# The down projection of narrow second tiles in plain float32 on groups of array columns

## The chip, the cores and the metric

The kernel runs on one core of a Trainium2 chip. The metric is the device time of one execution in microseconds (us), the median of several runs. Profiles are of one execution taken by the hardware profiler. Engines: PE is TensorE (PEld its weight loads), DVE is VectorE, ACT is ScalarE, POOL is GpSimd, SP is SyncE, which issues most of the transfers.

## The reference

One layer of a decoder over 4096 tokens of width 1024 in float32: a norm, a combined input projection, two groups of heads (gated DeltaNet and retention), an output projection with residual, and then a mixture of experts with residual and a last norm. The change lies in the mixture of experts alone:

```python
# top-1 group of 8, then top-2 of its 8 experts; 64 experts of width 256
gate = lax.ragged_dot(xs, w_gate, group_sizes)
up = lax.ragged_dot(xs, w_up, group_sizes)
y = lax.ragged_dot((jax.nn.silu(gate) * up).astype(xs.dtype), w_down, group_sizes)
y = y * weights[order].astype(y.dtype)[:, None]
out = jnp.zeros_like(ht).at[tok].add(y)
```

`w_down` is 256 x 1024 for each expert, so the contraction of the down projection has two slices of 128.

## The kernel before

The kernel runs through the mixer (both groups of heads), then `post` (the rest of the output projection, the router and a table of each expert's tokens), and last `moe`, the expert stage, from about 2700 us on.

Each expert has a fixed number of rows: the experts are ranked by their token counts, and rank r of either class gets `CAPS[r]` rows, from 256 down to 76. An expert with more than 128 rows has two tiles of rows, the first with 128 and the second with the rest. The second tiles have 128, 104, 84, 68, 60, 52, 48, 40, 32, 28, 24, 20, 16, 12, 8, 6, 4 and 2 rows, each size twice (one expert in each class). So 28 second tiles have at most 64 rows: 8 have 40 to 60, and 20 have 2 to 32.

The stage is written out by hand in rounds, one per expert e (`tc.manual_schedule()`, the loop at line 1650; the letters of `LOOP = "AFCDNBEGIMHJLO"` give the order). Every engine takes its instructions in that order. In round e, c is expert e, n is e+1, m is e+2, p is e-1 and q is e-2:

- A gathers the tokens of e+3 (POOL's queue); F gathers the rows of `out` of p (`gather_y`, POOL's queue).
- C and I are the gate and up products of c (`up`, line 1582), plain float32 with tiles of weights stationary and the tokens moving.
- D adds q's result (`add`), squares it on ScalarE (`square`), and has GpSimd take the power (`rms`); G norms and scatters it (`store`).
- B and H transpose n's first and second tile (`turn`, line 1512, with a product on VectorE at line 1514).
- N and E are the activation of c and p: `tanh`, then `silu`, which leaves h split into two float32r tiles `hh` and `hl`.
- M scales m's tokens on ScalarE. L prepares tables.
- J splits c's down weights: `split` (line 1399) makes `dh` on ScalarE and `dl` on VectorE from the raw float32 tile `dn`, then `fetch_dn(e)` asks for the down weights of expert e+2.
- O is the down projection of p: `down` (line 1517) for each tile.

`Rows.down` takes two halves of 512 output columns. For each one `mm3` (line 933) issues three float32r products (hh x dh, hh x dl, hl x dh) for each of the two slices of the contraction, with the tokens' h stationary (128 rows of the array by R columns) and 512 weights moving; the result `y` is a PSUM tile of one bank, of which there are two, and ScalarE evacuates it into `ys` with the token's weight as scale (line 1525). The product of one tile therefore has 12 float32r products and two evacuations.

The raw down weights `dn` have two buffers (`NDN = 2`, 1 MB per expert): those of e+2 take the buffer of e as soon as it is split. The gate and up weights `gu` have five buffers of half an expert; a load waits until the up product that read the buffer is through (line 1394). Both kinds are issued on SyncE's queue, in the order of the program.

Of the kernel before, what the change touches and what calls it, by code (L numbers as in the profile page):

```python
# [17 lines left out]
P = 128  # L18
# [55 lines left out]
def mixer(tc, outer, banks, x, attn_norm, w_in, conv_a, a_log, dt_bias, norm_a, norm_b, cst, rope, mixed, clear, w_out, x1):  # L74
    """Both groups of heads. While the last chains of products run out, the first row blocks of the output
    projection take the room between them; returns that projection, to go on with."""
# [6 lines left out]
    with ExitStack() as ctx:  # L83
# [23 lines left out]
        # a pair of heads of the first kind takes 16 units of projections, so does one of the second  # L107
# [16 lines left out]
        def fetch(m):  # L124
            """A quarter of 256 columns of weights: two of the eight slices."""
            if m < len(quarters):
                src, c0, n, k = quarters[m]
                W = src.shape[-1]
                raws[m] = wp.tile([P, 2, 264], F32, name="wr", bufs=NWR)
                nc.sync.dma_start(raws[m][:, :, :n], rows(src, c0 + k * 2 * P * W, [[W, P], [P * W, 2], [1, n]]))  # L130
# [16 lines left out]
        class Lane:  # L147
            """Chains that run beside the projections, a step at a time."""
# [38 lines left out]
        def unit(u, evac, kind):  # L187
            """After unit u of four of a group of projections."""
            g = gi[0]
            act = dict(L=la.tick, E=evac or (lambda: None), T=later, S=lambda: split(4 * g + 5 + u), B=behind)  # L190
            for o in STEPS[kind]:
                act[o]()
            if u == 3:
                gi[0] += 1
# [77 lines left out]
        # normalised, transposed and split input rows  # L272
# [33 lines left out]
        def x_prep(r):  # L306
            """Closures for the ticks that bring in row block r."""
            box = []
            return [lambda: box.append(x_norm(r)), lambda: box[0] and box[0]()]
# [47 lines left out]
        with tc.manual_schedule():  # L357
# [26 lines left out]
            def setup(i):  # L384
                """What the first units of projections need and come with."""
# [14 lines left out]
            for sb in range(NS):  # L400
# [4 lines left out]
                for kind, pr in stages:  # L405
# [3 lines left out]
                    if kind == "a":  # L409
                        # gate (and, with the first pair, beta and alpha)  # L410
# [22 lines left out]
                        # q, k, v with conv and SiLU (times two), channels on partitions  # L433
# [50 lines left out]
class Out:  # L484
    """The output projection and the residual, a block of rows at a time."""
# [30 lines left out]
    def half(self, r, h):  # L516
        """Half of the columns; a generator of two steps."""
# [30 lines left out]
    def units(self, n):  # L548
        """The first n blocks, as far as they are asked for. At the end of a block the next one is turned, and of the
        one after it the first operand loaded."""  # L550
# [29 lines left out]
# order of the work around a unit of projections: L a step of the chain of the first kind, E the unit's own  # L580
# results, T what waits for other engines, S the next weights, B small things in the background
STEPS = dict(g="LTBES", h="LBST", t="ELSTB", r="EBLTS", v="SBLET", y="LETSB")
# steps of that chain at each unit, for both pairs of heads
# [5 lines left out]
def zero(nc, t, zt, i, n):  # L589
    """Fill the i-th of n parts of a DRAM tensor with zeros."""  # L590
# [5 lines left out]
def gdn_pair(tc, sb, pr, co, gcd, gs, qkv, ready, L):  # L596
# [81 lines left out]
    # inverse of the unit upper triangular matrices: the diagonal blocks by substitution, NQ partitions to a block  # L678
    # with one of NQ rows in turn each, ...
# [49 lines left out]
    # ... then by block doubling  # L729
# [25 lines left out]
    # sequential part  # L755
# [120 lines left out]
# The groups are dealt to two classes by their number of tokens, and the experts of a class ranked by theirs.  # L876
# An expert of one class follows one of the other, so that a token's two experts are never neighbours.
# Rows kept for the expert of rank r in its class; what exceeds them takes the loop at the end.
# a round of the loop over the experts, and the last rounds; the sizes of the pairs of experts: b big, s small
# [6 lines left out]
def pairs():  # L886
    """Ranks in both classes, in the order of the work: large and small ones in turn, small ones at the end."""
# [38 lines left out]
class Split:  # L926
    """hi/lo halves (12 bits each) of a float32 operand."""
# [13 lines left out]
class Shared:  # L941
    """Constants of the router and of the experts, and what the one finds out for the other."""
# [33 lines left out]
def post(tc, out, wrg, wre, sh, tab, then):  # L976
    """The rest of the output projection, router, and the table of each expert's tokens."""
    nc = tc.nc
    NR = out.x.shape[-2] // P
    with ExitStack() as ctx:  # L980
# [13 lines left out]
        with tc.manual_schedule():  # L994
# [7 lines left out]
            # blocks are turned for the router two at a time until they have caught up  # L1002
# [47 lines left out]
            def turn_x(end):  # L1050
# [16 lines left out]
                # the last four in twos  # L1067
# [37 lines left out]
def route(tc, t0, n, S, sh, rst, xT, wr, usb, oneb, oacc, oaf, tab, scat, pools):  # L1105
    """Groups, experts and weights of n blocks of tokens, entered in the table; a generator of its steps."""
# [27 lines left out]
    def top(v, other):  # L1134
        """The largest of eight, its place counted from the end (the first one wins) and mask; other work between."""
# [12 lines left out]
    def exps(v):  # L1148
        """One over the sum of the exponentials of v less its largest, as work for top()."""
# [88 lines left out]
def counts(nc, psm, oneb, oacc):  # L1238
    """Tokens of each expert, along the rows and down a column."""
# [6 lines left out]
def place(sh, cr, key):  # L1246
    """An expert's rank in its class by what cr and key hold, and its place in the order."""
# [9 lines left out]
def classes(tc, sh, oneb, oacc, psm, sp):  # L1257
    """Classes of the groups, and the experts that come first, from the tokens so far; a generator of its steps."""
# [8 lines left out]
    # class of each group by its rank: 0 1 1 0 0 1 1 0  # L1267
# [26 lines left out]
    # the largest and the smallest keep their places  # L1294
# [13 lines left out]
def rank(tc, sh, oneb, oacc, psm, sp):  # L1308
    """Experts by falling count."""
# [21 lines left out]
def beyond(nc, sh, info, ptr):  # L1331
    """The list of tiles beyond the fixed ones: expert, first row."""
    C, io, q = sh.C, sh.io, sh.q
    cc = lambda i: q[:, i:i + 1]
    # tiles over the capacity, first of them
# [26 lines left out]
def moe(tc, w_gate, w_up, w_down, sh, x1, tab, info, out):  # L1362
    """The experts; a generator that leaves off once the first weights are asked for."""
# [5 lines left out]
    NX, NGU, NDN = 12, 5, 2  # L1369
    assert max(sum(NTILE[i:i + 6]) for i in range(NEXP)) <= NX  # L1370
    with ExitStack() as ctx:
# [6 lines left out]
        class Weights:  # L1378
            """An expert's weights, loaded in thirds."""
# [35 lines left out]
        def fetch_dn(e):  # L1415
            while dq and dq[0] <= e + NDN:
                W[dq.pop(0)].fetch(2)
# [3 lines left out]
        fetch_dn(-1)  # L1421
# [7 lines left out]
        def meta(M, n, selfkey, mask):  # L1429
            """Gather and scatter indices and scales of n tiles from their table rows."""  # L1430
# [12 lines left out]
            # the partner's place and capacity, and whether it lies beyond that  # L1443
# [11 lines left out]
            # second: the token's other expert comes before this one  # L1455
# [7 lines left out]
            # a first row stays scaled until it is stored  # L1463
# [22 lines left out]
        class Rows:  # L1486
            """Up to 128 tokens of an expert. A token's first expert leaves y + x1 in out, its second one
            adds to that and normalises."""
# [28 lines left out]
            def down(self, w, h, o):  # L1517
                R = self.R
                self.y = ap.tile([P, D], F32, name="ys")
                for c in range(2):  # L1520
# [3 lines left out]
                                     Split(w.hi[:, k, s], w.lo[:, k, s])) for k in range(2)])  # L1524
# [37 lines left out]
        class Expert:  # L1562
# [30 lines left out]
            def silu(self):  # L1593
# [6 lines left out]
                self.h = Split(hi, lo)  # L1600

            def down(self):
                for i, t in enumerate(self.tiles):
                    t.down(self.w.dn, self.h, i * P)
# [19 lines left out]
        with tc.manual_schedule():  # L1624
# [25 lines left out]
            for e in range(NEXP + 2):  # L1650
# [20 lines left out]
                def down_weights():  # L1671
                    c.w.split()
                    fetch_dn(e)

                def aside():
                    if e >= 8:
                        next(extra, None)
                    if e - e % G + G < NEXP:
                        if e % G < 4:
                            next(pend)  # L1680
                        elif e % G == 4:
# [5 lines left out]
                             M=(m, lambda: m.each("scale")), N=(c, lambda: c.tanh()), O=(p, lambda: p.down()))  # L1687
# [82 lines left out]
```

## Time and profile before

| | |
|---|---|
| time, median of 3 runs | 3663.53 us (3661.81 to 3665.11) |
| span of the profiled execution | 3669.7 us (the profile gives no other time for it) |
| TensorE busy | 3431.1 us, 93% |
| VectorE busy | 2415.7 us, 66% |
| ScalarE busy | 1716.0 us, 47% |
| GpSimd busy | 1140.5 us, 31% |
| DMA traffic | 573.55 MB, mean 156 GB/s |
| mean granted clock of TensorE | 0.977 |

The span runs from the first to the last instruction. Busy times are over the whole span; the expert stage has other shares than the mixer, so the stage is read from windows. Matmuls are pipelined, and a matmul's duration in a row goes on beyond the start of the next one: what a product takes on TensorE is read from the distance between starts. A plain float32 product appears as two weight loads and two matmuls, a float32r one as one of each.

### The profile page before, as it was taken

To read this page: it belongs to the slowest core of one execution; us is meant where nothing else is said; L and a number is where in the kernel's file an instruction comes from. 1 tells how busy PE (TensorE), PEld (TensorE's weight loads), DVE (VectorE), ACT (ScalarE), POOL (GpSimd) and SP (SyncE) were. 2 spreads that over 40 slices of the span, in tenths; PEclk is the share of its full clock that TensorE was granted. 3 is DMA by queue.
4 is the path that set the end of the run, shared out by engine and by line. 5 is a ranking of instruction groups with operands and counts; after the bars stand their busy time and mean duration, and the time that the engine had idled before them with its cause. 6 is when DMAs were issued, how large, how long until landed. Compare 5 with 4: busy or idle time off the path is not lost. (4 is left out here: it accounts for less than half of the span.)

```text
span 3669.7 us, 66531 instructions
## 1 busy us (share of the span) xinstructions
PE 3431.1 (93%) x24177; PEld 3137.1 (85%) x24177; DVE 2415.7 (66%) x6134; ACT 1716.0 (47%) x3706; POOL 1140.5 (31%) x1384
## 2 busy tenths in 40 slices
PE   7999999999999999999998999999969999999997
PEld 6888888888898888998988988888858888888885
DVE  6677677677677677677676664443546667777765
ACT  4345344344344444444444432222236666776775
POOL 1322332332232232232341320211123444444453
PEclk9999999999999999999999999999979999999998
DMA  5435335335344344353353335333267898999996
GB/s 139 116 84 141 85 87 139 86 100 126 87 121 110 82 121 105 82 132 98 85 122 100 86 98 168 110 116 103 82 199 251 285 307 295 310 309 335 345 308 196
DMA packets 565562, 573.55 MB, mean 156 GB/s; under 512 B 202560, under 2 KB 508272, under 8 KB 565232
## 3 DMA queue, kind: packets, MB, share of 16 engines
q1 hardware_dynamic: 528864, 484.51, 45.5%
q0 software_dynamic: 34976, 84.20, 6.5%
q8 instruction: 192, 3.15, 0.3%
q14 instruction: 138, 1.13, 0.1%
q10 hardware_dynamic: 1392, 0.56, 0.1%
HBM read 498.09 MB, written 102.56 MB: 164 GB/s over the span
## 5 line engine op out<-in xcount | busy, mean ns | idle before, releaser
L217 PE MATMUL acc<-wh,hh 128*128 128x256 f32 (+1 forms) x2560 | 764.8, 299 | 106.0 <-ACT rv L821 70.5
L219 PE MATMUL acc<-wh,hl 128*128 128x256 f32 (+1 forms) x2560 | 737.4, 288 | 2.4 <-DVE hl L297 2.4
L218 PE MATMUL acc<-wl,hh 128*128 128x256 f32 (+1 forms) x2560 | 737.5, 288 | 0.3 <-DVE wl L142 0.2
L217 PEld LDWEIGHTS acc<-wh,hh 128*128 128x128 f32 x2560 | 500.6, 196 | 116.3 <-ACT rv L821 73.8
L219 PEld LDWEIGHTS acc<-wh,hl 128*128 128x128 f32 x2560 | 500.2, 195 | 3.1 <-DVE hl L297 3.1
L218 PEld LDWEIGHTS acc<-wl,hh 128*128 128x128 f32 x2560 | 501.2, 196 | 1.0 <-DVE wl L142 0.8
L141 ACT ACTIVATE wh<-wr 128x512 fp32r<-128x512 f32 (+1 forms) x520 | 319.3, 626 | 252.0 <-DMA wr<-in_w_in_dram 247.5
L142 DVE TENSOR_TENSOR wl<-wr,wh 128x512 fp32r<-128x512 f32 (+1 forms) x520 | 388.0, 750 | 56.6 <-ACT wh L141 50.8
L205 PE MATMUL acc<-hh,wh 128*128 128x512 f32 x768 | 317.2, 413 | 0.0
L207 PE MATMUL acc<-hh,wl 128*128 128x512 f32 x768 | 303.3, 395 | 0.0
L206 PE MATMUL acc<-hl,wh 128*128 128x512 f32 x768 | 302.1, 393 | 0.0
L1582 PEld LDWEIGHTS g<-xT,gu 128*128 128x128 f32 x2048 | 273.4, 193 | 18.7 <-DVE xT L1514 9.2
L1582 PE MATMUL g<-xT,gu 128*128 128x128 f32 (+30 forms) x2048 | 279.1, 295 | 6.1 <-DVE xT L1514 6.0
L1582 PE MATMUL u<-xT,gu 128*128 128x128 f32 (+30 forms) x2048 | 275.6, 293 | 0.0
L1582 PEld LDWEIGHTS u<-xT,gu 128*128 128x128 f32 x2048 | 266.1, 191 | 1.9
L253 POOL TENSOR_TENSOR gs<-gs,nrow 128x256 f32<-128x256 f32 x128 | 118.6, 929 | 394.9 <-DVE gs L252 394.9
L245 DVE SCALAR_TENSOR_TENSOR cv<-xin,pcol,cv 128x512 f32<-128x512 f32 x288 | 216.0, 750 | 6.8
L810 POOL TENSOR_TENSOR rqk<-rqk,rb 128x256 f32<-128x256 f32 x128 | 118.3, 924 | 272.6 <-DVE rb L809 196.4
L1557 POOL DMA_INDIRECT out_dram<-xg,mi x100 | 130.4, 1304 | 188.9 <-DVE ss L1553 96.3
L1525 ACT ACTIVATE ys<-y,mf 128x512 f32<-128x512 f32 (+22 forms) x200 | 133.6, 679 | 113.8 <-PE y L938 100.7
L936 PE MATMUL y<-dh,hh 128*128 128x512 f32 (+16 forms) x400 | 164.6, 412 | 22.6 <-ACT ys L1525 13.8
L1528 POOL DMA_INDIRECT xg<-out_dram,mi x97 | 97.0, 1001 | 256.2 <-PE tr L1512 43.9
(367 smaller groups left out, 8143.3 us busy)
## 6 DMA issues: line engine op xcount, KB each, us to landing
wr<-in_w_in_dram SPq DMA_DIRECT2D x480, 256.0 KB
gu<-in_w_gate_dram SPq DMA_DIRECT2D x128, 512.0 KB
gu<-in_w_up_dram SPq DMA_DIRECT2D x128, 512.0 KB
dn<-in_w_down_dram SPq DMA_DIRECT2D x64, 1024.0 KB
xi<-in_x_dram SPq DMA_DIRECT2D x64, 512.0 KB
mixed<-mx SPq DMA_DIRECT2D x128, 128.0 KB
out_dram<-zt SPq DMA_DIRECT2D x8, 2048.0 KB
xi<-mixed SPq DMA_DIRECT2D x32, 512.0 KB
```

The costliest lines, as they stand in the source:

```text
L141: nc.scalar.activation(h, r, AF.Copy)
L142: nc.vector.tensor_tensor(l, r, h.bitcast(F32), op=OP.subtract)
L205: nc.tensor.matmul(a, wh[:, s], hh[:, k, :], start=(k == 0), stop=False)
L206: nc.tensor.matmul(a, wh[:, s], hl[:, k, :], start=False, stop=False)
L207: nc.tensor.matmul(a, wl[:, s], hh[:, k, :], start=False, stop=(k == KC - 1))
L217: nc.tensor.matmul(a[:, :n], hh[:, k, s], wh[:, :n], start=(k == 0), stop=False)
L218: nc.tensor.matmul(a[:, :n], hh[:, k, s], wl[:, :n], start=False, stop=False)
L219: nc.tensor.matmul(a[:, :n], hl[:, k, s], wh[:, :n], start=False, stop=(k == KC - 1))
L245: nc.vector.scalar_tensor_tensor(cv, xin[:, j:j + T], tap(j), cv, op0=OP.mult, op1=OP.add)
L936: nc.tensor.matmul(out, a.hi, b.hi, start=(i == 0), stop=False)
L1525: nc.scalar.activation(self.y[:R, s], y[:R], AF.Copy, scale=self.f[:R, WT, self.n:self.n + 1])
L1582: nc.tensor.matmul(o[:, b, :R], self.w.gu[k // 4][:, k % 4, i * DE + b * P:i * DE + b * P + P], self.xT[:, k, :R], start=(k == 0), stop=(k ...
```

## The change

For a second tile (`o` is the row offset, 0 for the first tile) of at most 64 rows, the down projection takes h as plain float32 (`h.whole`, the tile that `silu` had split) and the raw float32 weights (`w.raw`). The array's 128 columns are taken as groups of m = 32 (up to 32 rows) or 64 columns, and the 1024 output columns are cut into as many parts of n = 256 or 512. Each part goes to another group of columns, and with it to other partitions of one PSUM tile. Slices of the contraction are the outer loop, groups the inner one. ScalarE evacuates each group from its partitions into the part of `ys`, so four evacuations of 256 columns or two of 512.

First tiles, wider second tiles and the loop for what exceeds the fixed rows run as before, so all down weights are still split. Since the raw weights are read by the down projection, they have three buffers, and the weights of e+2 are asked for after p's down projection instead of after c's split; three experts' down weights are asked for ahead of the stage instead of two.

```diff
-        NX, NGU, NDN = 12, 5, 2
+        NX, NGU, NDN = 12, 5, 3
...
         def fetch_dn(e):
-            while dq and dq[0] <= e + NDN:
+            while dq and dq[0] < e + NDN:
                 W[dq.pop(0)].fetch(2)
...
-        fetch_dn(-1)
+        fetch_dn(0)
...
             def down(self, w, h, o):
                 R = self.R
                 self.y = ap.tile([P, D], F32, name="ys")
+                if o and R <= 64:
+                    m = 32 if R <= 32 else 64
+                    n = D * m // P
+                    y = py.tile([P, T], F32, name="y")
+                    for k in range(2):
+                        for j in range(P // m):
+                            nc.tensor.matmul(y[j * m:j * m + R, :n], h.whole[:, k, o:o + R], w.raw[:, k, j * n:j * n + n],
+                                             start=(k == 0), stop=(k == 1))
+                    for j in range(P // m):
+                        nc.scalar.activation(self.y[:R, j * n:j * n + n], y[j * m:j * m + R, :n], AF.Copy,
+                                             scale=self.f[:R, WT, self.n:self.n + 1])
+                    return
                 for c in range(2):
                     y = py.tile([P, T], F32, name="y")
                     s = slice(c * T, c * T + T)
                     mm3(nc, y[:R], [(Split(h.hi[:, k, o:o + R], h.lo[:, k, o:o + R]),
-                                     Split(w.hi[:, k, s], w.lo[:, k, s])) for k in range(2)])
+                                     Split(w.dn.hi[:, k, s], w.dn.lo[:, k, s])) for k in range(2)])
...
                 self.h = Split(hi, lo)
+                self.h.whole = h
...
             def down(self):
                 for i, t in enumerate(self.tiles):
-                    t.down(self.w.dn, self.h, i * P)
+                    t.down(self.w, self.h, i * P)
...
                 def down_weights():
                     c.w.split()
+                    if not p:
+                        fetch_dn(e)
+
+                def down():
+                    p.down()
                     fetch_dn(e)
...
-                             M=(m, lambda: m.each("scale")), N=(c, lambda: c.tanh()), O=(p, lambda: p.down()))
+                             M=(m, lambda: m.each("scale")), N=(c, lambda: c.tanh()), O=(p, down))
```

## Rows read from the trace of the kernel before

**Rows 1.** Windows: length, busy us (instructions) of each engine, granted clock, DMA share, GB/s.
```profile
2950.00:3159.50 209.50, 207.01 (x1358) 184.22 (x1357) 147.26 (x294) 144.06 (x194) 90.00 (x93) 1.00 0.91 300
3159.50:3594.60 435.10, 419.96 (x2986) 363.73 (x2985) 308.59 (x595) 310.29 (x423) 206.48 (x198) 1.00 0.94 323
3534.80:3538.20 3.40, 3.40 (x10) 2.26 (x9) 3.37 (x7) 2.38 (x4) 2.00 (x2) 0.50 1.09 357
```
**Rows 2.** Waits of PE, 3159.5 to 3594.6: us in total, times, longest.
```profile
PE y L936 <- ACT ys L1525: 8.2, 9, 1.5
PE y L936 <- ACT hh L1598: 5.3, 4, 3.1
```
**Rows 3.** Waits of DVE, 3159.5 to 3594.6.
```profile
DVE ss L1545 <- ACT g L1541: 67.4, 48, 2.4
DVE ss L1553 <- POOL ss L1546: 29.0, 14, 4.8
DVE hl L1599 <- ACT hh L1598: 13.8, 28, 0.5
...
DVE xT L1514 <- PE tr L1512: 3.6, 6, 1.1
```
**Rows 4.** Waits of DVE, 2950 to 3159.5.
```profile
DVE ss L1545 <- ACT g L1541: 29.6, 20, 2.5
...
DVE hl L1599 <- ACT hh L1598: 6.8, 13, 0.6
DVE ss L1553 <- POOL ss L1546: 5.5, 4, 2.8
```
**Rows 5.** Timeline of PE around a 32-row tile: start, us, instruction.
```profile
3172.65 4.51 PE L1582 MATMUL g<-xT,gu 128*128 128x160 f32 x32
3176.99 1.04 PE L1512 MATMUL tr<-cst,xg 128*128 128x128 f32 x8
...
3185.54 0.39 PE L938 MATMUL y<-dh,hl 128*128 128x512 f32 x1
3185.77 0.39 PE L936 MATMUL y<-dh,hh 128*32 128x512 f32 x1
...
3188.32 0.40 PE L938 MATMUL y<-dh,hl 128*32 128x512 f32 x1
3188.55 0.69 PE L1582 MATMUL g<-xT,gu 128*128 128x156 f32 x4
```
**Rows 6.** Groups by form, ACT, 2830 to 3669: xcount, busy us, mean ns, idle before.
```profile
L1525 ACT ACTIVATE ys<-y,mf 32x512 f32<-32x512 f32 x4 | 2.7, 680 | 2.8 <-PE y L938 2.8
...
L1591 ACT ACTIVATE h<-g 128x256 f32<-128x256 f32 x4 | 1.5, 363 | 0.0
```
**Rows 7.** Timeline of PE's weight loads, the same tile.
```profile
3185.55 0.11 PEld L936 LDWEIGHTS y<-dh,hh 128*32 128x32 f32 x1
3185.77 0.11 PEld L937 LDWEIGHTS y<-dl,hh 128*32 128x32 f32 x1
```
**Rows 8.** Timeline of ACT, the same tile.
```profile
3188.75 0.68 ACT L1525 ACTIVATE ys<-y,mf 32x512 f32<-32x512 f32 x1 [0.71 <-PE y L938]
3189.34 1.04 ACT L1541 ACTIVATE g<-xg 128x1024 f32<-128x1024 f32 x1
```
**Rows 9.** Waits of SP's queue, 2830.8 to 3594.6.
```profile
SPq L1394 <- PE u L1582: 313.1, 43, 11.9
SPq L1397 <- DVE dl L1403: 74.7, 23, 6.7
```
**Rows 10.** Timeline of SP's queue around the same tile.
```profile
3187.14 0.38 SPq L1397 DMA_DIRECT2D dn<-in_w_down_dram  x1
3197.04 0.37 SPq L1394 DMA_DIRECT2D gu<-in_w_gate_dram  x1
```
**Rows 11.** Timeline of PE ahead of a stretch at half clock.
```profile
3533.50 0.50 PE L936 MATMUL y<-dh,hh 128*128 128x512 f32 x1 [0.86 <-ACT hh L1598]
```

## Prediction

> **What bounds the kernel now.** The change touches only the expert stage, so I cut the view of windows there first. Narrow second tiles (at most 64 rows) come in two stretches: the 8 of 33 to 64 rows in 2950 to 3159.5 us, the 20 of at most 32 rows in 3159.5 to 3594.6 us, the last just behind it [rows 1]. The reader is to see TensorE busy 207.0 of 209.5 us and 420.0 of 435.1 us, DMA shares of 0.91 and 0.94, VectorE and ScalarE near 70%, and a granted clock of 1.00 in both (2.4 GHz). Next the waits of TensorE in the second stretch: 8.2 us for the evacuation `ys`, 5.3 us for `hh`, hardly anything else, no DMA [rows 2]. So TensorE sets the time, and what it saves is worth something. How much, the waits of VectorE tell. In the second stretch VectorE is busy 308.6 us, and waits 67.4 us for ScalarE's squares, 29.0 us for GpSimd's power and 13.8 us for `hh`, against only 3.6 us for TensorE [rows 3]. The first three are the replies of its own chain (add, square, power, norm), which a shorter product doesn't shorten. 308.6 + 67.4 + 29.0 + 13.8 = 418.8 of 435.1 us: VectorE's chain has about 16 us left before it is the bound. In the first stretch it is 147.3 + 29.6 + 6.8 + 5.5 = 189.2 of 209.5 us, 20 us left [rows 1, 4].
>
> **What is removed.** A narrow tile now takes 12 float32r products of 512 columns. With a 32-row tile the first starts at 3185.77 and the next expert's first product at 3188.55, so 2.78 us, 0.23 us each [rows 5]; there is no gap in it, all of it is on TensorE's path. The two evacuations of 512 columns cost ScalarE 0.68 us each [rows 6], 1.36 us.
>
> **What is added on TensorE.** A plain float32 product runs as two passes: the 16 products of `g` (8 slices, 2 halves) show as x32 [rows 5]. At 160 columns 32 passes take 3176.99 - 3172.65 = 4.34 us, 0.136 us each, so I estimate 0.136 x 256/160 = 0.217 us for 256 columns and 0.434 us for 512.
> - At most 32 rows: 2 slices x 4 groups x 2 passes = 16 passes of 256 columns, 16 x 0.217 = 3.47 us if one follows the other.
> - 33 to 64 rows: 2 x 2 x 2 = 8 passes of 512 columns, 8 x 0.434 = 3.47 us.
>
> So the work is longer by 0.69 us a tile unless passes in different groups of array columns run beside each other. No row of before has two groups at work, so it must be bounded. Upper end: no overlap, 3.47 us. Lower end: all groups together, 2 x 2 passes of one group: 0.87 us at 32 rows, 1.74 us at 64. Between them is the order in which the program issues: both passes of a product stand next to each other and go to the same group. In all rows here products start in program order. If that stays so, a second pass waits for the first of its group, and the first pass of the next group can start only beside it. Then 8 products at 32 rows take 9 steps of 0.217, 1.95 us, and 4 products at 64 rows 5 steps of 0.434, 2.17 us. I take this middle, since start in program order is what the rows show: saved 0.83 x 20 = 16.6 us in the second stretch and 0.61 x 8 = 4.9 us in the first, 21.5 us of TensorE.
>
> Two rules of the Trainium skill speak against the change. Going from 128 to 32 stationary columns and back costs nothing here: 3185.54 to 3185.77 and 3188.32 to 3188.55 are the same 0.23 us [rows 5]. The Trainium skill, "TensorEngine Tiling (Array Packing)", Key Properties, says that a change of the tiling mode drains the engine. Taken as the part of a product that lies beyond its spacing, 0.39 - 0.23 = 0.16 us, twice a tile, that would take 28 x 0.32 = 9.0 us off the saving; going by the row it is 0, and I keep the row, which has no column group other than the first in it. The weight loads of 0.11 us start at 3185.55 and 3185.77, beside products on the same rows of the array [rows 5, 7]. The Trainium skill, "TensorE: Matmul & The Clock Gate", Part 3, The mechanism, lets a load run beside a product only where the row groups differ; here all rows are used, and by it 16 x 0.11 = 1.8 us a tile would come on top. The trace disagrees, and I add nothing.
>
> **What is added elsewhere.** ScalarE: at 32 rows four evacuations of 256 columns take the place of two of 512. The nearest row, 256 columns out of PSUM, is 0.363 us; the other end is 0.68 us [rows 6]. I take 0.45, near the first, so 1.8 against 1.36 us, +0.44 us; range +0.1 to +1.36. It matters only for order: all four can start only after the last pass, where before one of two ran beside the products. Before, the last `ys` starts 0.20 us behind the products (3188.75 against 3188.55), and the next expert's square follows it at 3189.34 [rows 5, 8]. So ScalarE is through 0.20 + 0.68 = 0.88 us behind them, and after the change 0.20 + 4 x 0.45 = 2.00 us, 1.1 us later (two of 512 at 33 to 64 rows: 1.56 us, 0.7 later). Against the earlier end of the products this is 0.3 us lost at 32 rows and 0.1 at 64 for VectorE's chain. PSUM: one `y` buffer instead of two a narrow tile; the wait for the first tile's evacuation (8.2 us, rows 2) stays. ScalarE's and VectorE's splits of the weights stay too, for the first tiles.
>
> The weights' load: with three raw buffers the load for expert e+2 reuses the buffer of e-1, and is issued behind the products of e-1 rather than behind the split of e. SyncE now waits 74.7 us in all for that split (`dl`) [rows 9]. After the change it waits for the end of the down projection instead, at about the same place in a round (the products end at 3188.55, the load went out at 3187.14 [rows 5, 10]), and where the second tile isn't narrow, for nothing. Queued behind it are the next `gu` loads, which wait for `u` anyway (313.1 us, rows 9), at 3197.04, so some 8 us later. Cost 0; what hides it is that this load has nearly two rounds before its split. The third load ahead of the stage moves 1 MB earlier, off the path.
>
> **The sum.** Second stretch: 16.6 us are saved on TensorE, but VectorE's chain has 16 us of room and loses 20 x 0.3 = 6 us of it to the later squares, so 10 us. First stretch: 4.9 us saved, 20 us of room, 8 x 0.1 = 0.8 us lost, so 4 us. Together 14 us. The profiled execution gives its span alone, 3669.7 us; the median of the runs is 6.2 us below it (0.17%). The difference is carried over: 3663.5 - 14 = 3649.5 us.
>
> **Rivals.**
> - Full overlap: 1.91 x 20 + 1.04 x 8 = 46.5 us of TensorE. For it: groups write disjoint PSUM partitions and hold their own weights. Against it: the starts in program order. VectorE's chain caps the second stretch at 16 us, and the first leaves all 8.3 us: 24 us, 3639.5 us. The Trainium skill, "TensorE: Matmul & The Clock Gate", Part 3, Measured speedup vs the span model, gives 2.38 times for three column tiles; no row of before shows it.
> - No overlap, slower: the column groups take turns as products of the whole array do now. Place: every narrow tile. Price 0.69 x 28 = 19.3 us. TensorE's idle time (15 us in the second stretch, rows 1) takes in a few: +16, 3680 us. It decides from an overlap of less than 3.47 / 2.78 = 1.25. For it: no row of before shows two passes at once.
> - The chain of VectorE is already the bound in these rounds: TensorE only waits longer for `hh`; within 3 us of before, 3662 us.
> - The clock: soon after TensorE had waited 0.86 us for `hh` [rows 11], the granted clock stood at 0.50 (1.2 GHz) for 3.4 us [rows 1], which costs 1.7 us. If longer waits bring this in each of the 28 rounds, 48 us go, more than is saved: 3690 us with the saving of the middle case, 3663.5 + 48 - 21.5. Against it: it came once in 644 us.
>
> **How the numbers follow.** Middle case 42%, full overlap 24%, no overlap 20%, chain of VectorE 9%, clock 5%. About 0.2% (7.3 us) can be told from no change. The middle case lies between 4 and 20 us faster and reaches the bound in three of four; full overlap nearly always; no overlap nearly always on the other side. Faster: 0.32 + 0.23 = 0.55; slower: 0.18 + 0.05 = 0.23; the rest, 0.22, within. The range must reach to no overlap on one side and into full overlap on the other: 3633 to 3680 us; the middle case alone is 3644 to 3660.
>
> **What would show it.** In the trace after, a narrow tile's passes: starts 0.217 us apart mean no overlap, pairs at 0.217 us the middle, four starts close together full overlap; first pass to the next expert's `g` in 3.5, 2.0 or 0.9 us. Wrong on the sum if VectorE's waits for TensorE stay at a few us while TensorE's waits for `hh` grow by as much as it saves (VectorE bound), or if stretches at clock 0.50 become frequent, or if `dn` loads are late and ScalarE waits for them.

## The result and the profile after

The kernel after takes 3695.03 us (median; 3691.41 to 3697.2) against 3662.89 us for the one before on the same chip: the ratio is 1.0075, 95% interval 1.0063 to 1.0088. The forecast was 3649.5 us with a range of 3633 to 3680. The sign was wrong and the time lies outside the range.

What the change does on TensorE, it does better than forecast. The timeline of PE around a 32-row tile and a 60-row tile in the kernel after (start, us, instruction; xN counts passes), beside [rows 5]:

```profile
3194.71 0.39 PE L938 MATMUL y<-dh,hl 128*128 128x512 f32 x1
3195.03 1.07 PE L1527 MATMUL y<-dn,h 128*32 128x256 f32 x16
3196.03 2.25 PE L1595 MATMUL g<-xT,gu 128*128 128x156 f32 x15
...
2987.70 0.39 PE L938 MATMUL y<-dh,hl 128*128 128x512 f32 x1
2988.02 1.94 PE L1527 MATMUL y<-dn,h 128*60 128x512 f32 x8
2989.89 3.82 PE L1595 MATMUL g<-xT,gu 128*128 128x104 f32 x32
```

From the wide tile's last product to the next expert's first it is 3196.03 - 3194.71 = 1.32 us (2.19 us for the 60-row tile), where the kernel before needs 3188.55 - 3185.54 = 3.01 us [rows 5]. Where nothing waits, that is 1.69 us saved in each of 20 tiles and 0.82 us in each of 8, 40 us in all. And yet the kernel lost 32 us.

The windows of [rows 1] in the kernel after, and a stretch of 3.3 us further on (length, busy us of PE, PEld, DVE, ACT and POOL, granted clock, DMA share, GB/s). Of TensorE's 435.1 us, 392.8 are busy:

```profile
2950.00:3159.50 209.50, 204.58 (x1341) 178.90 (x1339) 145.70 (x286) 144.93 (x194) 89.90 (x92) 0.99 0.92 303
3159.50:3594.60 435.10, 392.80 (x2970) 346.03 (x2969) 303.17 (x591) 314.94 (x451) 206.07 (x195) 0.97 0.92 316
...
3351.90:3355.20 3.30, 3.23 (x8) 2.56 (x9) 1.75 (x3) 3.21 (x5) 2.13 (x4) 0.50 1.10 358
```

Waits of PE in 3159.5 to 3594.6 us, kernel after (us in total, times, longest), which answer to [rows 2]. The wait for `hh` went from 5.3 to 16.5 us, and waits for `xT`, 0.5 us before, come to 13.8 us:

```profile
PE y L936 <- ACT hh L1611: 16.5, 14, 5.5
PE y L1527 <- ACT ys L1538: 11.6, 11, 1.5
PE tr L1512 <- DVE xT L1514: 6.9, 10, 2.6
PE g L1595 <- DVE xT L1514: 6.9, 7, 2.1
```

Waits of DVE in 3159.5 to 3594.6 us, then in 2950 to 3159.5 us, kernel after, which answer to [rows 3, 4]. VectorE's wait for GpSimd's power is what grew: 29.0 to 46.2 us, and 5.5 to 14.7 us. Its wait for TensorE's transposes, 3.6 us before, is 0.3 us in the second stretch: there VectorE no longer waits for TensorE, TensorE waits for VectorE.

```profile
DVE ss L1558 <- ACT g L1554: 63.8, 49, 2.1
DVE ss L1566 <- POOL ss L1559: 46.2, 19, 5.2
DVE hl L1612 <- ACT hh L1611: 14.9, 30, 0.5
...
DVE xT L1514 <- PE tr L1512: 0.3, 1, 0.3
...
DVE ss L1566 <- POOL ss L1559: 14.7, 5, 4.7
```

Waits of SP's queue in 2830.8 to 3594.6 us, kernel after, which answer to [rows 9]. The down-weight load (L1397) waited 74.7 us for `dl`, the split of this round; now it waits for the end of the narrow products in some rounds, and in most for nothing:

```profile
SPq L1394 <- PE u L1595: 385.6, 47, 16.7
SPq L1397 <- PE y L1527: 68.2, 18, 9.8
SPq L1397 <- DVE dl L1403: 16.4, 3, 6.3
```

One round shows the whole chain. Timelines of SP's queue, POOL, DVE and PE in the kernel after, 3324 to 3352 us (start, us, instruction; in brackets the idle time before it and what the profile infers as its end):

```profile
3324.67 0.37 SPq L1394 DMA_DIRECT2D gu<-in_w_up_dram  x1
3325.29 0.66 SPq L1397 DMA_DIRECT2D dn<-in_w_down_dram  x1
...
3326.26 2.06 POOL L1570 DMA_INDIRECT out_dram<-xg,mi  x1 [1.93 <-DVE xT L1514]
3328.62 1.93 POOL L1501 DMA_INDIRECT xg<-x,mi  x1 [0.30 <-issue]
3336.32 0.99 POOL L1541 DMA_INDIRECT xg<-out_dram,mi  x1 [5.76 <-ACT xg L1505]
3337.62 0.95 POOL L1541 DMA_INDIRECT xg<-out_dram,mi  x1 [0.30 <-ACT dh L1402]
3338.60 0.59 POOL L1559 TENSOR_TENSOR ss<-ss,ex 128x1 f32<-128x1 f32 x1
...
3330.93 0.15 DVE L1558 TENSOR_SCALAR ss<-ss 128x1 f32<-128x1 f32 x1 [1.27 <-ACT g L1554]
3339.22 0.28 DVE L1566 TENSOR_SCALAR ss<-ss,mf 128x1 f32<-128x1 f32 x1 [5.17 <-POOL ss L1559]
3340.74 2.35 DVE L1403 TENSOR_TENSOR dl<-dn,dh 128x1024 fp32r<-128x1024 f32 x2
...
3350.03 0.42 PE L1512 MATMUL tr<-cst,xg 16*128 16x16 f32 x4 [2.61 <-DVE xT L1514]
3351.97 0.80 PE L936 MATMUL y<-dh,hh 128*128 128x512 f32 x1 [0.93 <-ACT hh L1611]
3352.57 0.63 PE L937 MATMUL y<-dl,hh 128*128 128x512 f32 x1
3352.99 0.63 PE L938 MATMUL y<-dh,hl 128*128 128x512 f32 x1
```

The 1 MB down-weight load is requested 0.62 us behind the last of the `gu` loads, and 1 us before the scatters of the finished rows (`out_dram<-xg`). The gather of `y` rows (`xg<-out_dram`) has by the program to wait for these scatters to land, and stands at the head of GpSimd's queue until 3336.32. The bracket there names an instruction of ScalarE (`xg`, line 1505) that the program has behind this gather; the scatter of 3326.26 landed at 3335.46 by the trace, 9.2 us after its start, and the gather waits on that scatter's semaphore. The power, whose operand VectorE had finished at 3331.08, is behind it in program order and starts at 3338.60. VectorE's norm waits 5.17 us for it, the work behind it on VectorE slides (the split of the down weights starts at 3340.74), and one round later TensorE waits 2.61 and 0.93 us. Then it runs on at the lower clock: the products of 512 columns start 0.42 us apart (3352.57 to 3352.99) instead of 0.23, and the window above has a granted clock of 0.50, 1.2 GHz.

Three numbers over the whole stage, worked out from the timelines (2715 to 3655 us), say that this is no single round:

- Scatters issued within 3 us behind the request of a down-weight load: 1 of 100 before, 33 of 97 after.
- From the last scatter of a round to the first gather of `y`: in the kernel after a median of 9.2 us where a down load was requested from 4 us ahead of the first of these scatters on (30 rounds), 7.8 us elsewhere (30 rounds). The trace gives a landing for 37 of the 97 scatters: the 20 of them with a request from 4 us ahead to 1 us behind took a median of 8.7 us to land, the other 17 took 7.2.
- From the end of VectorE's instruction that feeds a power to the power's start: a mean of 3.00 us before, 3.56 after.

### The profile page after: what moved, and what is told of

Its sections match the earlier page's. It is cut to its first block, busy times and chain, and to the rows that moved or that the text cites. A ratio compares the mean times of both kernels' runs of the same rounds, so it can differ in the third digit from the quotient of the medians.

```text
span 3693.9 us, 66686 instructions
## 1 busy us (share of the span) xinstructions
PE 3417.3 (93%) x24225; PEld 3131.8 (85%) x24225; DVE 2414.3 (65%) x6134; ACT 1730.0 (47%) x3746; POOL 1145.9 (31%) x1384
## 5 line engine op out<-in xcount | busy, mean ns | idle before, releaser
L1554 ACT ACTIVATE g<-xg 128x1024 f32<-128x1024 f32 x100 | 105.6, 1056 | 148.8 <-DVE xg L1549 133.0
L207 PEld LDWEIGHTS acc<-hh,wl 128*128 128x128 f32 x768 | 144.4, 188 | 33.9
```

Source lines behind the costliest of these rows:

```text
L207: nc.tensor.matmul(a, wl[:, s], hh[:, k, :], start=False, stop=(k == KC - 1))
```

## The experiments

In the table below, scatters behind a load are those of the first bullet, power is the mean delay of the third; idle is TensorE's time in gaps of over 0.5 us between starts (each less one spacing of 0.23 us), and half the time at 1.2 GHz, both from the first expert's first `g` product to the last expert's (63 rounds). Ratios are to the kernel before, run on the same chip.

| kernel | ratio (95%) | scatters behind a load | power, us | idle, us | half, us |
|---|---|---|---|---|---|
| before | 1 | 1 of 100 | 3.00 | 32 | 12 |
| after | 1.0075 (1.0063 to 1.0088) | 33 of 97 | 3.56 | 71 | 63 |
| e1 loads alone | 1.0088 (1.0071 to 1.0105) | 44 of 96 | 3.88 | 50 | 25 |
| e2 products again | 1.0089 (1.0072 to 1.0106) | 30 of 97 | 3.24 | 45 | 29 |
| e3 loads held | 0.9979 (0.9969 to 0.9990) | 0 of 100 | 2.78 | 52 | 32 |
| e4 held alone | 1.0004 (0.9992 to 1.0016) | 0 of 100 | 2.79 | 29 | 14 |
| e5 = e1, gather later | 1.0001 (0.9989 to 1.0012) | 37 of 100 | 0.25 | 26 | 12 |
| e6 = e3, gather later | 0.9959 (0.9948 to 0.9970) | 1 of 100 | 0.20 | 43 | 19 |
| e7 = after, gather later | 0.9977 (0.9964 to 0.9990) | 27 of 100 | 0.18 | 45 | 18 |
| e8 = before, gather later | 0.9984 (0.9974 to 0.9994) | 1 of 100 | 0.22 | 25 | 9 |
| e9 = e6, narrow tile first | 1.0046 (1.0033 to 1.0059) | 0 of 98 | 0.18 | 68 | 46 |
| e10 = e7, narrow tile first | 1.0076 (1.0063 to 1.0089) | 46 of 98 | 0.22 | 71 | 49 |
| e11 = e6, narrow tile between | 0.9989 (0.9978 to 1.0001) | 0 of 100 | 0.20 | 48 | 46 |
| e12 = e7, split behind | 1.0432 (1.0415 to 1.0449) | 11 of 84 | 0.15 | 150 | 206 |

The columns say how a saving of 40 us becomes a loss. In the profiled runs, from before to after, the 63 rounds get longer by 20.2 us (917.6 to 937.8): TensorE idles 39 us more, and 51 us more at 1.2 GHz cost some 25, together 64, less the 40 saved; that closes within 4 us.

**e1: the load part alone, on the kernel before.**

```diff
-    NX, NGU, NDN = 12, 5, 2
+    NX, NGU, NDN = 12, 5, 3
...
-            while dq and dq[0] <= e + NDN:
+            while dq and dq[0] < e + NDN:
...
+                    if not p:
+                        fetch_dn(e)
+
+                def down():
+                    p.down()
                     fetch_dn(e)
...
```

> Theory A (TensorE's saved time turns into waits, since the chain of VectorE, GpSimd and the scatters sets the rounds, and the waits drop the granted clock to 0.50 in more stretches: 48 us of half clock in the stage after, 3.4 before): the third raw buffer and the later place of the load request alone do nothing, 3656 to 3670 us, half clock in the stage at most 7 us. Theory B (the down weights are now asked for right behind the gate and up weights, so their transfers run beside the scatters and gathers, these land later, and GpSimd's power and VectorE's norm with them): slower by most of what after lost, 3680 to 3695 us, VectorE's waits for the power near 80 us as after.

Measured: 3698.93 us, 1.0088. The whole loss is here, without a single column group. Waits of DVE, 2715 to 3655 us, first in the kernel before, then in e1:

```profile
DVE ss L1553 <- POOL ss L1546: 46.1, 28, 4.8
```
```profile
DVE ss L1553 <- POOL ss L1546: 81.7, 35, 5.1
```

35.6 us more of waiting for the power stand against 31 us of time. With 25 us at half clock in 63 rounds against 63 in the kernel after, the loss is the same; the 13 us more than before cost some 6 of the 31 us, so the low clock doesn't make most of it.

**e2: the kernel after with TensorE's saving taken back**: the narrow products are issued three times (at 33 to 64 rows one and a half times), so that a tile takes about 2.7 us again. The first product of each repetition starts the sum anew, so the result stays the same and only work is added.

```diff
-                    for k in range(2):
+                    for k, first, last in [(k, k == 0, k == 1) for k in 2 * [0, 1] + [0, 1]] if m == 32 else [
+                            (0, True, True), (0, True, False), (1, False, True)]:
```

> After, with each narrow tile's products issued three times (at most 32 rows) or one and a half times (33 to 64), so that TensorE takes about 2.7 us for such a tile as before; loads as after. Theory A: the waits and most half-clock stretches go, 3656 to 3672 us, half clock in the stage under 12 us. Theory B: the loads are still early, 3685 to 3700 us.

Measured: 3696.82 us, 1.0089. Time at half clock falls from 63 to 29 us and the total doesn't move. With the early loads, 40 us of TensorE more or less are worth 0.14% or nothing (the intervals overlap). Nor are dips of the clock the cause: 34 us less of them leave the time where it was.

**e3: the kernel after with the load held back** by a store of 4 bytes that has to wait for this round's split, as the load itself does before the change.

```diff
+        hold = ctx.enter_context(tc.tile_pool(name="hd", bufs=1, space=DRAM)).tile([P, 4], F32, name="hold")
...
                 def down():
                     p.down()
+                    if c:
+                        nc.sync.dma_start(hold[0:1, 0:1], c.w.dn.lo[0:1, 1, D - 1:D].bitcast(F32))
                     fetch_dn(e)
```

> After, with a store of 4 bytes from the split weights of this round ahead of the request, so that the load of the down weights waits for that split as before; narrow products as after. Theory A: no help, 3685 to 3697 us, half clock in the stage 35 to 60 us. Theory B: 3640 to 3665 us, VectorE's waits for the power back near 46 us.

Measured: 3659.73 us, 0.9979. No scatter is issued close behind a load any more, and the wait for the power is 39.0 us in place of 79.9 (waits of DVE, 2715 to 3655 us, in the kernel after, then in e3):

```profile
DVE ss L1566 <- POOL ss L1559: 79.9, 33, 5.2
```
```profile
DVE ss L1567 <- POOL ss L1560: 39.0, 25, 3.2
```

Holding one load for some microseconds turns 0.75% slower into 0.2% faster.

**e4: the control, held loads and three buffers without the groups**: e1 with e3's edit.

```diff
-    NX, NGU, NDN = 12, 5, 2
+    NX, NGU, NDN = 12, 5, 3
...
+                def down():
+                    p.down()
+                    if c:
+                        nc.sync.dma_start(hold[0:1, 0:1], c.w.dn.lo[0:1, 1, D - 1:D].bitcast(F32))
                     fetch_dn(e)
...
```

> The kernel before with three raw down-weight buffers, the down products as before, and the 4-byte store that makes the down-weight load wait for this round's split (as in e3). It is the control for e3: the difference between the two is the column groups alone. Theory B (only the early load costs) expects 0.998 to 1.003 of before, so the groups in e3 are worth 0 to 0.4%, and waits of VectorE for the power at 40 to 50 us in all. Rival: three buffers or the store cost something themselves (the load goes out later than in before, because the store has to come first), then 1.004 or more here, and the groups are worth more than e3 against before shows.

Measured: 3666.27 us, 1.0004, as expected of the theory of the loads (the wait for the power is 38.3 us, just under its 40 to 50). Three buffers and the store cost nothing that can be told, and the groups in e3 are worth 0.25% (0.9979 against 1.0004), some 9 us. Views of DMA issues, 2715 to 3640 us (KB each, median us to landing), of e1, then of e4:

```profile
dn<-in_w_down_dram SPq DMA_DIRECT2D x60, 1024.0 KB, 12.0
...
out_dram<-xg,mi POOLq DMA_INDIRECT x94, 8.6
```
```profile
out_dram<-xg,mi POOLq DMA_INDIRECT x98, 7.3
```

The scatters land 1.3 us later where the load goes out ahead of them (8.0 us in the kernel after, 7.0 in e3). These medians are over the issues whose landing the trace gives: 74 of the scatters in e1, 64 in e4, 37 in the kernel after, and only 7 of the loads in e1.

**e5: e1 with the gather behind the power** on GpSimd: step F (gather of `y` rows) is issued behind step D (add, square, power).

```diff
-LOOP, TAIL = "AFCDNBEGIMHJLO", "BLCEFDGHIMNAOJ"
+LOOP, TAIL = "ACDFNBEGIMHJLO", "BLCEDFGHIMNAOJ"
```

> e1 (the loads alone) with the gather of y rows issued behind the power in GpSimd's order instead of ahead of it (step F behind D in the loop). Theory M1: the early load makes the scatters land late, the gather waits for them at the head of GpSimd's queue, and the power stands behind it; then taking the power ahead of the gather gives back most of the 31 us: 3663 to 3678 us, and VectorE's wait for the power falls from 81.7 us to under 40. Rival M2: what is late is data itself (scattered and gathered rows land later, and the add waits for them), so the order on GpSimd does not matter: 3690 to 3710 us, with VectorE waiting for the gather in the add instead.

Measured: 3665.27 us, 1.0001. All of the loss is gone, though 37 of 100 scatters still follow close behind a load and land after 7.8 us. Waits of DVE in e5, 2715 to 3655 us:

```profile
DVE ss L1553 <- POOL ss L1546: 1.5, 2, 0.8
...
DVE xg L1536 <- DMA xg<-out_dram,mi: 28.3, 15, 4.9
```

So M1 holds: the price is mostly not the later landing itself, but that the power stands in line behind the gather that waits for it. M2 has a small part: the add now waits 28.3 us for gathered rows, and against e8 below, which has the same order without the early load, e5 is 0.17% longer (1.0001 against 0.9984), some 6 us, at the edge of what the intervals tell.

**e6, e7 and e8: the same order with the held load, on the kernel after, and on the kernel before**, by the edit of e5 each time.

```diff
-LOOP, TAIL = "AFCDNBEGIMHJLO", "BLCEFDGHIMNAOJ"
+LOOP, TAIL = "ACDFNBEGIMHJLO", "BLCEDFGHIMNAOJ"
```

> e3 (the groups, the load held) with the gather behind the power. M1: the wait for the power that is left in e3 (38 us) shrinks to under 25 us, and TensorE's gaps with it: 3640 to 3655 us. Rival M2: no gain, or the add is late because the gather goes out later: 3658 to 3675 us.

> The changed kernel itself with the gather behind the power and nothing else; early load as it is. M1: the loss goes, and the groups' saving of some 43 us of TensorE can show: 3640 to 3665 us, clock dips fewer (under 20 us at half clock), the power's wait under 40 us. Rival M2: 3690 us or more.

> The kernel before with nothing changed but the gather of y rows behind the power in GpSimd's order. Control for e6 and e7. Theory: in before the power's 46 us of waits are partly the same effect, but little of it reaches TensorE there (TensorE waits 15 us for other engines' results, apart from evacuations), so 0.998 to 1.000; then the groups' own gain in e7 against this is 0.2 to 0.4%. Rival: the order alone gives what e6 shows, 0.996 to 0.997, and the groups give nothing in any form.

Measured: e6 3651.28 us (0.9959), e7 3657.85 us (0.9977), e8 3665.08 us (0.9984; the chip gave 3671.39 us for the kernel before in that series). e7 differs from the kernel after in the place of one letter in each of the two orders, and is 1% faster than it. e6 is the fastest version found and beats both kernels. The order alone is worth 0.16% (e8). The groups are worth 0.25% on top of it with held loads (e6 against e8) and 0.24% with early ones (e7 against e5), some 9 us in both pairs, as in e3 against e4. The early load still costs 0.18% in e7 against e6, about as in e5 against e8, both at the edge of the intervals. In the profiled runs the accounts of e8 and e6 close: from e8 to e6 the 63 rounds get shorter by 17.0 us (907.7 to 890.7), idle time grows by 18.6, and 9.8 us more at half clock cost some 5; together 40.5, the 40 us that TensorE saves. More than half is given back, as waits and as time at the low clock. Which waits, the view of PE says (2715 to 3655 us), first in e6, then in e8; a single wait of 16.5 us in e6 lies ahead of the first round:

```profile
PE y L936 <- ACT hh L1612: 15.0, 13, 5.1
PE y L1528 <- ACT ys L1539: 14.6, 15, 1.5
```
```profile
PE y L936 <- ACT hh L1598: 3.4, 3, 1.8
```

So the wait for `hh` is the one that grows; that for `ys` was 14.8 us in e8. And VectorE waits only 1.8 us for transposes in 3159.5 to 3594.6 us of e6. That fits a bound outside TensorE, but not the prediction's cap as it was worked out. Window (as in [rows 1]) and waits of DVE in 3159.5 to 3594.6 us of e8, then waits of DVE in e6:

```profile
3159.50:3594.60 435.10, 422.59 (x3026) 366.90 (x3024) 314.18 (x599) 315.87 (x432) 220.80 (x202) 1.00 0.95 328
DVE ss L1545 <- ACT g L1541: 69.8, 49, 2.6
DVE hl L1599 <- ACT hh L1598: 10.3, 21, 0.5
...
DVE xT L1514 <- PE tr L1512: 6.0, 10, 1.2
```
```profile
DVE xg L1550 <- DMA xg<-out_dram,mi: 12.8, 8, 6.0
DVE dl L1403 <- ACT dh L1402: 7.1, 7, 1.1
```

The wait for the power, 29.0 us in [rows 3], is gone from this stretch in e8. The prediction's sum is then 314.2 + 69.8 + 10.3 = 394.3 us, or 402 us with two waits of 8.0 us in all on the same lines for which the view has no releaser: more than 30 us of room instead of 16, in this stretch alone. Yet the groups gave the same 9 us. The sum leaves out what else VectorE waits for, in e6 gathered rows and ScalarE's half of the split; its waits for TensorE, which a shorter product can take away, are only 6.0 us in e8 and 1.8 in e6. Three more orders were tried to get at TensorE's waits for `hh` and `ys`; none gained: they made these waits worse or moved them.

**e9 and e10: the narrow tile ahead of the wide one** (on e6 and on e7).

```diff
-                for i, t in enumerate(self.tiles):
+                ts = list(enumerate(self.tiles))
+                if len(ts) > 1 and ts[1][1].R <= 64:
+                    ts.reverse()
+                for i, t in ts:
                     t.down(self.w, self.h, i * P)
```

> e6 with the narrow tile's products ahead of the wide tile's. They need only the float32 h, not the split hh, and they leave one buffer of PSUM free for the wide tile, whose first evacuation no longer stands ahead of them. In e6 TensorE waits 15.0 us for hh and 14.6 us for that evacuation (2715 to 3655 us). Theory C (TensorE is still the bound in these rounds, and what is left of the 43 us it saves is lost in these two waits): both shrink to under half, 3630 to 3645 us. Rival D (VectorE's own chain is the bound, as the prediction's cap said): TensorE only waits elsewhere (for xT and h), 3647 to 3656 us, no gain over e6's 0.9959.

> The same order of tiles on e7 (early load, gather behind the power). Theory C: 3638 to 3652 us, 5 to 15 us below e7; rival D: as e7, 3653 to 3662 us. Whichever holds, the early load is expected to cost 3 to 10 us against e9, as e7 stood against e6.

Measured: 1.0046 and 1.0076, slower by 0.9 and 1.0% than e6 and e7. Neither theory said so. Waits of PE in e9, 2715 to 3655 us:

```profile
PE y L936 <- ACT ys L1531: 49.4, 22, 3.6
...
PE y L936 <- ACT hh L1612: 1.4, 3, 1.0
```

The wait for `hh` goes, as theory C wanted, but the wide tile's second half now needs the buffer of PSUM that the narrow tile's four evacuations hold, 49.4 us in 22 waits; VectorE's add waits longer for the wide tile's rows too (57.1 us for `ys` in place of 11.3). So the four small evacuations, 4 x 0.468 us, cost more here ahead of the wide tile's than behind them.

**e11: the narrow tile between the wide tile's halves** (on e6).

```diff
-            def down(self, w, h, o):
+            def down(self, w, h, o, cs=(0, 1)):
...
-                for c in range(2):
+                for c in cs:
...
+                if len(self.tiles) > 1 and self.tiles[1].R <= 64:
+                    a, b = self.tiles
+                    a.down(self.w, self.h, 0, (0,))
+                    b.down(self.w, self.h, P)
+                    a.down(self.w, self.h, 0, (1,))
+                    return
```

> e6 with the narrow tile's products between the two halves of the wide tile's. In e9 TensorE lost 49.4 us waiting for the narrow tile's four evacuations, since the wide tile's second half needed their buffer; here it needs the buffer of the wide tile's first half instead, which stands ahead of them on ScalarE. Theory C (what e9 lost is that buffer): most of the 49 us goes, the time comes back to e6's 0.996 within 0.2%; the wait for the first half's evacuation is 15 to 25 us, since only the 1 us of the narrow products covers it, where 1.4 us did in e6. Rival D (the new order as such is bad, since the wide tile's rows reach VectorE's add later): 1.002 or more.

Measured: 3665.68 us, 0.9989 (0.9978 to 1.0001), between the two theories. Waits of PE and of DVE in e11, 2715 to 3655 us:

```profile
PE y L936 <- ACT ys L1540: 24.1, 19, 1.9
...
DVE xg L1551 <- ACT ys L1540: 32.5, 23, 3.1
```

The buffer's wait falls from 49.4 to 24.1 us, as C said; but the add waits 32.5 us for `ys`, which is D's point, and it is 0.3% slower than e6. In the profiled runs its rounds are 18.3 us longer than e6's (3.5 us of that in the first round), of which idle time makes 4.3 us, and 26.5 us more at half clock some 13. It doesn't settle how much belongs to each theory.

**e12: the split of the down weights behind the down products** (step J behind O in the loop, on e7).

```diff
-LOOP, TAIL = "ACDFNBEGIMHJLO", "BLCEDFGHIMNAOJ"
+LOOP, TAIL = "ACDFNBEGIMHLOJ", "BLCEDFGHIMNAOJ"
```

> e7 with ScalarE's and VectorE's split of the down weights issued behind the down products instead of ahead of them. In e7 TensorE waits 17.2 + 3.8 us for ys with the 2 us split ahead of the evacuations on ScalarE. Theory C (these waits are what is left to gain): they fall under 6 us and the time to 0.993 to 0.996. Rival D (ScalarE and VectorE only have the split in the way elsewhere, ahead of the next round's square and add): the waits for ys go, those for hh and xT grow, 0.997 to 1.005.

Measured: 3826.89 us, 1.0432; D's direction, ten times its size. Waits of DVE in e12, 2715 to 3655 us:

```profile
DVE dl L1403 <- ACT dh L1402: 190.9, 44, 8.7
```

TensorE's waits for `ys` go, as D said, and those for `hh` (51.9 us) and `xT` (51.6 us) grow. ScalarE's half of the split now stands behind the evacuations, which wait for TensorE, and VectorE's half stands at the head of VectorE's queue until it is done. It is of the kind of e1, on another engine: an instruction that waits blocks what is behind it. Part of the price is the low clock, 206 us at 1.2 GHz in these rounds against 18 in e7.

## Why the prediction was wrong

- **The step that failed is the weights' load, costed at 0.** Alone it cost 31 us (e1), the whole of the loss. The prediction said that the load goes out "at about the same place in a round" and that nearly two rounds before its split hide it. The second is so: where the trace of the kernel after gives a landing (16 of 60 loads here) the load takes a median of 10.1 us and lands at least 12 us ahead of its split, and in no round does the split wait for a load. The first isn't: the median distance behind the last `gu` request fell from 3.4 to 0.95 us (0.62 in e1). What counts is not when this load has to land but what its 1 MB stands ahead of: the scatters of that round. I asked who waits for the load; I should have asked also who shares the DMA engines with it (share 0.94 in [rows 1]), and which queue waits for those transfers. The order on GpSimd, gather ahead of power, was there to be read in the program, and VectorE's wait for the power in [rows 3], 4.8 us at the longest, was the mark of it. I had counted those 29.0 us as a reply of VectorE's own chain that stays; with the gather behind the power they are gone (e8), so they were time in GpSimd's queue, and it could grow.
- **Passes on TensorE.** I gave the middle 42% and full overlap 24%; full overlap it is: 0.98 to 1.00 us from the first pass to the next `g` for 16 passes in 15 of the 20 tiles (0.9 was the mark; the other five take 1.08 to 3.16), 1.87 for 8 (1.74). In the trace four passes start within 0.02 us, and the fifth 0.24 us behind the first (PE, 3195.0 to 3195.21 us, kernel after):

```profile
3195.03 0.42 PE L1527 MATMUL y<-dn,h 128*32 128x256 f32 x4
```

So a second pass that waits for the first of its group doesn't keep back the other groups, though I had it do so; whether the passes stood in another order than I took, the rows don't say, as they don't name the group of a pass. In e2 a tile's 48 passes take 2.71 us, so 16 more cost 0.86 us, the 0.87 of full overlap. The Trainium skill, "TensorE: Matmul & The Clock Gate", Part 3, Measured speedup vs the span model, gives 2.38 times for three column tiles; four here make 3.47 / 0.98 = 3.5 times by my single-pass estimate. As for the drain on a change of tiling, the first pass starts 0.32 us behind the last wide product where 0.23 is the spacing, so 0.09 us on the way in; I had 0.
- **The cap by VectorE's chain** was right in that most of TensorE's saving is lost, and wrong in its working. In the kernel after the saving is worth nothing measurable (after against e1), and with the loads' harm taken away (e3 against e4, e6 against e8) 0.25%, some 9 us; full overlap was to give 24. The mark that I had named for it is in the rows: TensorE's wait for `hh` trebles, and VectorE hardly waits for TensorE. But the room of 16 us doesn't set the size: with the power's wait gone the same sum leaves more than 30 us, and the gain is no larger. Of the 16 us only 3.6 were a wait for TensorE's transposes [rows 3]; I took for room what VectorE spent on other waits and short gaps too. What holds e6 where it is stays open; no run took it apart.
- **ScalarE.** Four evacuations at 0.468 us each, 1.87 us; the estimate was 1.8.
- **The clock.** I gave dips 5% and 48 us. They came, nine stretches of 44 us in all between 2715 and 3640 us against one of 3.4 us before (beside the one that the stage starts in, 19.0 and 7.4 us), but behind waits that had another cause; e2 has two of them and the same time.
- **The cases.** The loss has a mechanism that none of the five had. The case nearest in time, no overlap (3680 us), has the opposite of what TensorE did; the one nearest in kind, VectorE's chain as the bound, had it unchanged at 3662 us, where GpSimd made that chain longer.

## What to carry to other kernels

A load that is requested earlier is not free because it is needed late: look at what else is issued in the microseconds behind it, and at which in-order queue waits for that. Take out of such a queue's way, by program order alone, a short instruction that others wait for; here one letter's place in each order was worth 1%. And when an edit of one engine comes with a change of a transfer's place, time each by itself, since a saving of 40 us on one engine, worth 9 us here, can hide behind 30 us that have nothing to do with it.

## What the runs showed of the hardware

Four groups of 32 array columns run float32 passes side by side almost without loss (16 passes in 0.98 to 1.00 us, where by my estimate one group's four take 0.87), and their weight loads, 128 rows high each, go along: 16 loads in 0.59 us of busy time in the view of PE's weight loads, around the first tile above:

```profile
3195.03 0.59 PEld L1527 LDWEIGHTS y<-dn,h 128*32 128x32 f32 x16 [0.35 <-issue]
```

A scatter of rows issued close behind the request of a 1 MB load landed later (8.7 against 7.2 us in the kernel after, 8.6 in e1 against 7.3 in e4), which put the next gather off from 7.8 to 9.2 us. The kernel before has one such round only (6.6 us, against 8.1 elsewhere). Why the order on the DMA engines does so was not looked into.
